# Rotary angle tables computed on GpSimd, their sines placed amid the chunks, and the second projection unit's weight splits put late and on VectorE, in a planned hybrid attention block

## The chip, the cores and the metric

The kernel runs on one core of a Trainium2 chip. The metric is the device time of one execution in microseconds. The profile is one further execution of the same program.

The engines are named as the profile names them: PE is TensorE (matmuls; PEld is its weight load), DVE is VectorE, ACT is ScalarE, POOL is GpSimd, and SP is SyncE, which issues the transfers. Each engine runs its own instructions strictly in the order in which they stand.

## What is computed

One decoder layer on x of 1024 tokens by 1024 features, in float32:

```python
mod = silu(c) @ w_ada + b_ada
sh_a, sc_a, gt_a, sh_m, sc_m, gt_m = split(mod, 6)
h = rms_norm(x, g_attn_pre) * (1 + sc_a) + sh_a
proj = h @ w_in
qa, ka, va, qb, kb, vb = split(proj)
qa, ka, qb, kb = partial_rope(each, cos, sin)
oa = banded_attention(qa, ka, va, 127, sink)
ob = dilated_mixture_attention(qb, kb, vb)
y = concat(rms_norm(oa), rms_norm(ob)) @ w_out
x = x + gt_a * rms_norm(y)
h = rms_norm(x) * (1 + sc_m) + sh_m
x = x + gt_m * rms_norm(square(relu(h @ w_up)) @ w_down)
```

`cos` and `sin` are those of position times eight fixed frequencies. They turn the first 16 of each head's 64 dimensions.

## The kernel before, in words

**Precision.** A matmul takes operands rounded to fp32r. The kernel keeps each operand as a high part (a rounding copy on ACT) and a low part (a subtraction on DVE or POOL, original minus high part) and multiplies high by high, high by low and low by high. So every weight and activation tile is "split": one ACT instruction, then one on DVE or POOL.

**A planner sets the order.** The function `hybrid_block` does not issue instructions directly. It hands steps to `Sched` with `op`: an engine (or two to choose from), an assumed duration in microseconds, the code that emits the instructions, the steps it depends on, counted resources that it takes and gives (`takes`, `gives`: buffers of a ring, PSUM banks), and a priority. `Sched.run` plays a clock forward and always places the step that can start first, so the assumed durations and the dependencies decide the order on every engine. For a step with two engines it picks the one that would end it first. On the chip each engine then runs its fixed list, with semaphores between the engines.

**x phase (x_block, lines 574 to 597).** Eight blocks of 128 tokens of x arrive. For each one ACT squares it with a row sum (L578); DVE scales the sum (L417, `rs_t`); POOL takes the power of minus one half (L420, `rstd`); DVE or ACT multiplies the block by it (L584 or L583, below "the scaling"); PE transposes it in two groups of four (L591), and DVE or ACT copies each group from PSUM into `xnT` (L595).

**Chunk phase (mod_chunk, lines 601 to 628).** Feature chunk k (of 8) of the normalized activations needs a scale `g_a` and a shift `s_a`. DVE computes each by a 1024-long product with row sum (L606, below "the gemv", two per chunk), ACT then writes the chunk's high part `hw` (L618) and the full value (L621), and DVE the low part (L624). With these goes the split of the first unit's weights for chunk k: ACT L490, DVE L495.

**The projection.** It has six units of 384 columns. In the first unit (`first_unit`) PE takes the chunks as they come: for each of chunks 0 to 5, all eight token blocks into eight accumulators `acc`, first two matmuls of each block with the high part (L747, L748) and then one with the low part (L750). Chunks 6 and 7 follow together, token block by token block. The other units (`proj_tile`, PSUM tiles `pj`) go token block by token block over all eight chunks, one set of three matmuls (L747, L748, L750) per chunk. `next_unit_w` asks for a unit's weights, and `split_w` (lines 487 to 501) splits them; for units 1 to 5 the low part could be on DVE or POOL.

**Evacuation of a projected block (evac, lines 646 to 740).** ACT writes the high part of v (L660), DVE its low part (L665); DVE turns the rotary dimensions by `cosw` and `sinw` (L676, L678, L680, below "the turn"); ACT and DVE split q and k (`sp`, `sk`: L687, L688; L692, L693); PE transposes them (`pq` L700, `pk` L712) through the one PSUM bank `px`; ACT writes `qt` (L705) and ACT or DVE `kt` (L726). Then scores (`s_ps`, L975), minimum with mask (L993, DVE), exponential (L1000, ACT), reciprocal (L1003, DVE) and normalization (L1005, POOL) follow.

**Rotary tables.** Eight angles for each of the 8 x 128 positions are 64 elements per partition. A product (L553), two rounds of range reduction (L556, L557, and L559 with L560 for each of 12 parts of two pi) and four closing steps (L566 to L569) make `ang` and `kq`, all on DVE with low priority (8); two sines on ACT (L636, L637) follow behind `e_full`, which is the last chunk's full value, and a negation on DVE (L640). The exponential in L638 only brings the table of the exponential back.

## Time and profile before

| what | us |
|---|---|
| three timed runs | 1180.21, 1184.89, 1187.25 |
| their median | 1184.89 |
| the profiled execution | 1177.44 |
| its span in the trace | 1175.3 |
| PE busy in the span | 1121.8 |
| DVE, ACT, POOL busy | 885.0, 670.4, 232.2 |

The profiled execution's time is 2.1 us more than its span, and 7.5 us less than the median of the three timed runs.

A row of the timeline has the start, the duration, the engine, the line in the code, the operation, the output and input tiles with shapes, and a count where equal neighbours are merged; in brackets stands how long the engine sat idle just before, and what ended the wait. Starts follow each other more closely than durations say, since an instruction's tail overlaps the next. A row of the windows view has, for a stretch of time, the busy time of PE, PEld, DVE, ACT and POOL with their instruction counts, then the granted PE clock (1.00 is full speed), the DMA share and GB/s.

### The profile page before, as it was taken

Reading aid. Unit: us, or ns where it says so; the run is one execution under the profiler, and the core shown is the slowest. Engines: PE = TensorE matmul, PEld = TensorE weight load, DVE = VectorE, ACT = ScalarE, POOL = GpSimd, SP = SyncE. Lnnn points to the kernel's source line nnn. Section 1 sums busy time; section 2 is a strip of 40 time slices with the busy share of each in tenths; the row PEclk is TensorE's granted clock in tenths of the full one; section 3 lists DMA queues with packets and bytes.
Section 4 is the critical chain, followed back from the end, with each engine's and each line's share of the span. In section 5 each row is a group of like instructions: output and inputs, shape, how many; then the busy total and the mean of one; then the engine's idle time right before and its main releaser. Section 6 shows DMA issues by size and latency. Waiting matters only on the chain.

```text
span 1175.3 us, 17156 instructions
## 1 busy us (share of the span) xinstructions
PE 1121.8 (95%) x5964; PEld 975.4 (83%) x5964; DVE 885.0 (75%) x1812; ACT 670.4 (57%) x1400; POOL 232.2 (20%) x279
## 2 busy tenths in 40 slices
PE   5889999999999989999899999999999999999996
PEld 4889999899988877888688888888888888888885
DVE  8978787676798986668979765489653796636998
ACT  7767666565667776667667524473225733246542
POOL 2334474554744341111000000000000000000002
PEclk9989999999999999999999999999999999999998
DMA  9602223132223224465485147932268411575103
GB/s 338 230 31 78 77 84 117 53 97 84 76 59 110 82 64 126 154 205 226 144 334 191 36 139 257 337 100 90 93 221 304 143 47 54 202 287 198 37 19 143
DMA packets 77542, 166.51 MB, mean 142 GB/s; under 512 B 6800, under 2 KB 27408, under 8 KB 77456
## 3 DMA queue, kind: packets, MB, share of 16 engines
q1 hardware_dynamic: 77456, 165.42, 41.3%
q8 instruction: 47, 0.77, 0.3%
q14 instruction: 39, 0.32, 0.1%
HBM read 137.08 MB, written 28.31 MB: 141 GB/s over the span
## 4 chain that ended last, share of the span: by engine, by line
PE 62%; DVE 10%; ACT 3%; issue 3%; POOL 2%; DMA 1%; SPq 0%; DVEq 0%; POOLq 0%; ACTq 0%
PE mlp_ps L1751 16%; PE mlp_ps L1752 16%; PE mlp_ps L1750 16%; PE pj L747 2%; PE pj L750 2%; PE pj L748 2%; PE s_ps L975 1%; DMA o_sb<-o_dram 1%; DVE hw L1521 1%; PE y_ps L1326 1%; PE y_ps L1328 1%; PE o_ps L1120 1%; PE y_ps L1327 1%; DVE x_sb L1852 1%; DVE ph L1096 1%
## 5 line engine op out<-in xcount | busy, mean ns | idle before, releaser
L1750 PE MATMUL mlp_ps<-hw 128*128 128x512 f32 x896 | 349.7, 390 | 1.2 <-ACT hw L1512 1.2
L1751 PE MATMUL mlp_ps<-hw 128*128 128x512 f32 x896 | 348.7, 389 | 1.1 <-DVE hw L1518 1.1
L1752 PE MATMUL mlp_ps<-hw 128*128 128x512 f32 x896 | 348.6, 389 | 0.0
L1750 PEld LDWEIGHTS mlp_ps<-hw 128*128 128x128 f32 x896 | 168.2, 188 | 36.8 <-ACT hw L1512 1.6
L1751 PEld LDWEIGHTS mlp_ps<-hw 128*128 128x128 f32 x896 | 168.2, 188 | 36.7 <-DVE hw L1518 1.4
L1752 PEld LDWEIGHTS mlp_ps<-hw 128*128 128x128 f32 x896 | 168.2, 188 | 34.9
L1521 DVE TENSOR_TENSOR hw<-w,hw 128x1024 fp32r<-128x1024 f32 x96 | 114.7, 1223 | 91.7 <-ACT hw L1514 91.5
L1514 ACT CAST hw<-w 128x1024 fp32r<-128x1024 f32 x96 | 97.4, 1046 | 129.8 <-PE mlp_ps L1752 97.5
L1850 POOL TENSOR_TENSOR st<-st,nhalf 128x1 f32<-128x1 f32 x8 | 7.8, 978 | 601.9 <-DVE st L1848 601.9
L747 PE MATMUL pj<-w_hl,hw 128*128 128x384 f32 x320 | 118.3, 370 | 4.6 <-DVE sk L693 4.6
L750 PE MATMUL pj<-w_hl,hw 128*128 128x384 f32 x320 | 108.1, 338 | 0.0
L748 PE MATMUL pj<-w_hl,hw 128*128 128x384 f32 x320 | 107.9, 337 | 0.0
L1514 ACT CAST hw<-u 128x1024 fp32r<-128x1024 f32 x48 | 48.7, 1052 | 64.6 <-PE mlp_ps L1752 64.6
L1096 DVE TENSOR_TENSOR ph<-pt_ps,ph 128x512 fp32r<-128x512 f32 (+1 forms) x110 | 69.1, 644 | 18.3 <-ACT ph L1092 17.8
L1521 DVE TENSOR_TENSOR hw<-u,hw 128x1024 fp32r<-128x1024 f32 x48 | 57.1, 1221 | 18.2 <-ACT hw L1514 18.2
L1005 POOL TENSOR_SCALAR p_sb<-p_sb,den 128x128 f32<-128x128 f32 (+3 forms) x64 | 49.3, 774 | 93.4 <-DVE den L1003 69.7
L1092 ACT CAST ph<-pt_ps 128x512 fp32r<-128x512 f32 (+1 forms) x110 | 59.5, 560 | 12.6 <-PE pt_ps L1081 8.7
L747 PEld LDWEIGHTS pj<-w_hl,hw 128*128 128x128 f32 x320 | 60.4, 189 | 6.3 <-issue 2.9
L1808 DVE TENSOR_TENSOR yacc<-yacc,mlp_ps 128x512 f32<-128x512 f32 x96 | 62.2, 684 | 3.3 <-PE mlp_ps L1752 3.3
L1000 ACT ACTIVATE p_sb<-p_sb,mn 128x128 f32<-128x128 f32 (+3 forms) x64 | 50.0, 781 | 21.8 <-DVE mn L993 17.8
L748 PEld LDWEIGHTS pj<-w_hl,hw 128*128 128x128 f32 x320 | 60.6, 189 | 1.2 <-issue 0.2
L750 PEld LDWEIGHTS pj<-w_hl,hw 128*128 128x128 f32 x320 | 60.1, 188 | 0.0
(205 smaller groups left out, 2176.8 us busy)
## 6 DMA issues: line engine op xcount, KB each, us to landing
hw<-s_dram SPq DMA_DIRECT2D x84, 512.0 KB, 4.5
wa_st<-in_w_ada SPq DMA_DIRECT2D x32, 512.0 KB, 4.1
w<-in_w_up SPq DMA_DIRECT2D x32, 512.0 KB, 4.9
w<-in_w_down SPq DMA_DIRECT2D x32, 512.0 KB, 7.8
s_dram<-hw SPq DMA_DIRECT2D x28, 512.0 KB, 5.0
w_st<-in_w_in SPq DMA_DIRECT2D x48, 192.0 KB, 3.8
x_sb<-in_x SPq DMA_DIRECT2D x16, 512.0 KB, 5.2
wa<-in_ada_t SPq DMA_DIRECT2D x16, 512.0 KB, 8.0
```

The lines of the kernel that those rows point to most:

```text
L747: T.matmul(ps, hw[:, tb, 0, t], w[:, 0], start=(k == 0), stop=False)
L748: T.matmul(ps, hw[:, tb, 0, t], w[:, 1], start=False, stop=False)
L750: T.matmul(ps, hw[:, tb, 1, t], w[:, 0], start=False, stop=(k == KC - 1))
L1000: A.activation(rec.p[qi], rec.p[qi], AF.Exp, bias=b["mn"][:, m:m + 1], scale=-1.0, accum_out=b["den"][:])
L1092: A.copy(b["ph"][:, 0, :w], b["pt"][:, :w])
L1096: V.tensor_tensor(b["ph"][:, 1, :w], b["pt"][:, :w], b["ph"][:, 0, :w].bitcast(F32), ALU.subtract)
L1514: A.copy(out[j][0], flat(src[j]))
L1521: V.tensor_tensor(out[j][1], flat(src[j]), out[j][0].bitcast(F32), ALU.subtract)
L1750: T.matmul(ps[m][:], sh, mh, start=starts and k == 0, stop=False, **kw)
L1751: T.matmul(ps[m][:], sh, ml_, start=False, stop=False, **kw)
L1752: T.matmul(ps[m][:], sl, mh, start=False, stop=k == 3, **kw)
L1808: e = op("DVE", t_dv(512), lambda: V.tensor_tensor(y(), y(), ps[m][:], ALU.add), [e, ml.e_y[tb, n]], gives=gives, prio=1)
```

## The change

It has five edits:

1. The range reduction of the rotary angles moves from DVE to POOL, instruction by instruction, with an assumed 0.38 us each; of the four closing steps only the clamp remains there (L569 of the changed file).
2. ACT takes over the rest: a sine with scale minus one replaces the negation, an absolute value (L638) and a sine with bias pi/2 replace the three other closing steps. The block stands behind the full value of chunk 4 instead of 7, with priority 0.
3. The low part of unit 1's weights goes to DVE alone, and waits for the low part of the last chunk (`e_hl[KC - 1]`).
4. The assumed cost of the POOL power goes from 0.18 + 0.165 w to 0.4 + 0.165 w, and that of the square to 1.14.
5. One more small constant is set at the start (`halfpi`).

```diff
-        return op("POOL", 0.18 + 0.165 * w, lambda: G.tensor_tensor(dst, box[0][:, :w], nhalf[:, :w], ALU.pow),
+        return op("POOL", 0.4 + 0.165 * w, lambda: G.tensor_tensor(dst, box[0][:, :w], nhalf[:, :w], ALU.pow),
...
+        elif u == 1:
+            w_e[u, k] = op("DVE", t_dv(UW), lo(V), [e, e_hl[KC - 1]], gives=[(r_wst, 1)], prio=3)
...
-    steps = [lambda: V.tensor_tensor(ang[:], posf[:].unsqueeze(2).to_broadcast([P, TB, 8]),
+    steps = [lambda: G.tensor_tensor(ang[:], posf[:].unsqueeze(2).to_broadcast([P, TB, 8]),
...
-            steps += [lambda part=part: V.tensor_scalar(km[:], kq[:], -part, 1.0, ALU.mult, ALU.mult),
-                      lambda: V.tensor_tensor(ang[:], ang[:], km[:], ALU.add)]
+            steps += [lambda part=part: G.tensor_scalar(km[:], kq[:], -part, 1.0, ALU.mult, ALU.mult),
+                      lambda: G.tensor_tensor(ang[:], ang[:], km[:], ALU.add)]
...
-        e = op("DVE", 0.12, f, [e, e_c], prio=8)
+        e = op("POOL", 0.38, f, [e, e_c], prio=8)
...
-        V.tensor_scalar(ang[:], ang[:], 3.1415925, -3.1415925, ALU.min, ALU.max)
-        V.tensor_scalar(kq[:], ang[:], -1.0, None, ALU.mult)
-        V.tensor_tensor(kq[:], kq[:], ang[:], ALU.max)
-        V.tensor_scalar(kq[:], kq[:], -1.0, float(np.pi / 2), ALU.mult, ALU.add)
-    e = op("DVE", 0.8, f_ang, [e], prio=8)
+        G.tensor_scalar(ang[:], ang[:], 3.1415925, -3.1415925, ALU.min, ALU.max)
+    e = op("POOL", 0.4, f_ang, [e], prio=8)
...
-        e = op("ACT", t_sb(D) + AP_COST, f_sq, [x_e[tb]], prio=2)
+        e = op("ACT", 1.14, f_sq, [x_e[tb]], prio=2)
...
         A.activation(sinw[:, :, 1], ang[:], AF.Sin)
-        A.activation(cosw[:], kq[:], AF.Sin)
-        A.activation(ang[:], kq[:], AF.Exp)
-    e = op("ACT", 3.0, f_sin, [e_ang, e_full[0]], prio=8)
-    e_rope = op("DVE", 0.15, lambda: V.tensor_scalar(sinw[:, :, 0], sinw[:, :, 1], -1.0, None, ALU.mult), [e],
-                prio=8)
+        A.activation(sinw[:, :, 0], ang[:], AF.Sin, scale=-1.0)
+        A.activation(kq[:], ang[:], AF.Abs)
+        A.activation(cosw[:], kq[:], AF.Sin, bias=halfpi[:], scale=-1.0)
+        A.activation(ang[:], kq[:], AF.Exp, scale=-1.0)
+    e_rope = op("ACT", 3.3, f_sin, [e_ang, e_full[4]], prio=0)
```

The planner then lays the instructions anew. Line numbers of the changed file are one to three higher around these places.

POOL's list at the start of the program, before: the eight powers `rstd` of the x phase stand first, and seven low parts of unit 1's weights follow.

```order
L420 ISA
L420 TENSOR_TENSOR rstd<-rs_t,nhalf 128x1 x8
L495 TENSOR_TENSOR w_hl<-w_st,w_hl 128x384 x7
L860 TENSOR_SCALAR ada_acc<-wa_st,cond 128x512
L864 TENSOR_SCALAR wa_st<-wa_st,cond 128x512
```

The same place now:

```order
L556 ISA
L556 TENSOR_TENSOR ang<-posf,head 128x64
L559 TENSOR_SCALAR kq<-ang 128x64
L560 TENSOR_SCALAR kq<-kq 128x64
L562 TENSOR_SCALAR km<-kq 128x64
L563 TENSOR_TENSOR ang<-ang,km 128x64
L562 TENSOR_SCALAR km<-kq 128x64
L421 TENSOR_TENSOR rstd<-rs_t,nhalf 128x1
L563 TENSOR_TENSOR ang<-ang,km 128x64
L562 TENSOR_SCALAR km<-kq 128x64
L563 TENSOR_TENSOR ang<-ang,km 128x64
L421 TENSOR_TENSOR rstd<-rs_t,nhalf 128x1
```

Six rotary instructions now stand ahead of the first power and 25 ahead of the eighth; five follow behind it. The seven splits of weights have left this place.

DVE's list where the last chunk is finished, before: `hw` is the low part of a chunk (the second one shown is the last chunk's), `w_hl_662` the one low part of unit 1 that DVE had, and the others are rotary steps.

```order
L624 TENSOR_TENSOR hw_126<-xnT_159,hw_126 128x8x128
L611 TENSOR_TENSOR g_a_72<-g_a_72,head_65 128x1
L559 TENSOR_SCALAR km_163<-kq_162 128x64
L495 TENSOR_TENSOR w_hl_662<-w_st_633,w_hl_662 128x384
L560 TENSOR_TENSOR ang_161<-ang_161,km_163 128x64
...
L569 TENSOR_SCALAR kq_162<-kq_162 128x64
L624 TENSOR_TENSOR hw_126<-xnT_159,hw_126 128x8x128
L640 TENSOR_SCALAR sinw_77<-sinw_77 128x8x8
```

The same place now. `w_hl_646` is the last split of unit 0, `w_hl_659`, `w_hl_672` and `w_hl_678` are chunks 0, 1 and 2 of unit 1; `acc_426` is the first token block that is evacuated.

```order
L624 TENSOR_TENSOR hw_127<-xnT_160,hw_127 128x8x128 x2
L496 TENSOR_TENSOR w_hl_659<-w_st_538,w_hl_659 128x384
L676 TENSOR_TENSOR ra_717<-acc_426,cosw_77 128x64
...
L496 TENSOR_TENSOR w_hl_672<-w_st_548,w_hl_672 128x384
...
L993 ISA mn_920 128x1
L496 TENSOR_TENSOR w_hl_678<-w_st_582,w_hl_678 128x384
L496 TENSOR_TENSOR w_hl_705<-w_st_640,w_hl_705 128x384
```

The rotary steps are gone from between the last two low parts, and the splits of unit 1 stand behind the last one: two at the start of the evacuations, and six (`w_hl_678` is the first of them) behind all eight turns of unit 0. From the first set of unit 2's first token block on, the lists of PE before and now are the same to the end (4459 of 5072 rows), and those of the other engines are the same from the same part of the program on.

More of the change, by code (lines that the diff above doesn't have):

```diff
@@ L362, in hybrid_block @@
     nhalf = const.tile([P, KC], F32, name="nhalf")
+    halfpi = const.tile([P, 1], F32, name="halfpi")
     cond = const.tile([P, KC], F32, name="cond")
@@ L509, in hybrid_block @@
         load_w(0, k)
-    e_init = op("DVE", 0.3, lambda: (V.memset(ones[:], 1.0), V.memset(nhalf[:], -0.5)), prio=0)
+    e_init = op("DVE", 0.3, lambda: (V.memset(ones[:], 1.0), V.memset(nhalf[:], -0.5), V.memset(halfpi[:], float(np.pi / 2))), prio=0)
     e = op("ACT", 0.1, lambda: A.activation(cond[:], c_raw, AF.Exp, scale=-1.0), [e_c], prio=0)
@@ L552, in hybrid_block @@
     km = p0.tile([P, TB, 8], F32, name="km")
-    steps = [lambda: V.tensor_tensor(ang[:], posf[:].unsqueeze(2).to_broadcast([P, TB, 8]),
+    steps = [lambda: G.tensor_tensor(ang[:], posf[:].unsqueeze(2).to_broadcast([P, TB, 8]),
                                      inv_f.unsqueeze(1).to_broadcast([P, TB, 8]), ALU.mult)]
     for inv, parts in ((1.0 / (TWO_PI * 4096), COARSE), (1.0 / TWO_PI, FINE)):
-        steps += [lambda inv=inv: V.tensor_scalar(kq[:], ang[:], inv, ROUND, ALU.mult, ALU.add),
-                  lambda: V.tensor_scalar(kq[:], kq[:], -ROUND, 1.0, ALU.add, ALU.mult)]
+        steps += [lambda inv=inv: G.tensor_scalar(kq[:], ang[:], inv, ROUND, ALU.mult, ALU.add),
+                  lambda: G.tensor_scalar(kq[:], kq[:], -ROUND, 1.0, ALU.add, ALU.mult)]
         for part in parts:
-            steps += [lambda part=part: V.tensor_scalar(km[:], kq[:], -part, 1.0, ALU.mult, ALU.mult),
-                      lambda: V.tensor_tensor(ang[:], ang[:], km[:], ALU.add)]
+            steps += [lambda part=part: G.tensor_scalar(km[:], kq[:], -part, 1.0, ALU.mult, ALU.mult),
+                      lambda: G.tensor_tensor(ang[:], ang[:], km[:], ALU.add)]
     e = e_pos
     for f in steps:
-        e = op("DVE", 0.12, f, [e, e_c], prio=8)
+        e = op("POOL", 0.38, f, [e, e_c], prio=8)
     def f_ang():
-        V.tensor_scalar(ang[:], ang[:], 3.1415925, -3.1415925, ALU.min, ALU.max)
-        V.tensor_scalar(kq[:], ang[:], -1.0, None, ALU.mult)
-        V.tensor_tensor(kq[:], kq[:], ang[:], ALU.max)
-        V.tensor_scalar(kq[:], kq[:], -1.0, float(np.pi / 2), ALU.mult, ALU.add)
-    e = op("DVE", 0.8, f_ang, [e], prio=8)
+        G.tensor_scalar(ang[:], ang[:], 3.1415925, -3.1415925, ALU.min, ALU.max)
+    e = op("POOL", 0.4, f_ang, [e], prio=8)
     e_ang = e
@@ L597, in x_block @@
                            gives=[(r_t, 1)], prio=2))
-    e_hh, e_hl, e_full = {}, {}, [None]
+    e_hh, e_hl, e_full = {}, {}, {}
     def mod_chunk(k):
@@ L625, in mod_chunk @@
         e_hh[k] = op("ACT", t_sb(S) + 2 * AP_COST, hi, [e1, e2] + e_xn, prio=0)
-        e = e_full[0] = op("ACT", t_sb(S) + 2 * AP_COST, full, [e_hh[k]], prio=0)
+        e = e_full[k] = op("ACT", t_sb(S) + 2 * AP_COST, full, [e_hh[k]], prio=0)
         e_hl[k] = op("DVE", t_dv(S), lo, [e], prio=0)
```

## Prediction

> **What bounds the kernel now.** I read the page, then the windows, then PE's waits and its timeline at the start, then DVE's and POOL's lists around the longest wait. PE bounds the kernel, and the start and one later stretch are where it doesn't run:
>
> ```profile
> span 1175.3 us, 17156 instructions
> ...
> PE 1121.8 (95%) x5964; PEld 975.4 (83%) x5964; DVE 885.0 (75%) x1812; ACT 670.4 (57%) x1400; POOL 232.2 (20%) x279
> ```
> ```profile
> 80.00:100.00 20.00, 17.47 (x142) 16.65 (x141) 17.20 (x65) 16.36 (x56) 5.59 (x9) 1.00 0.05 11
> ...
> 100.00:152.00 52.00, 52.00 (x385) 50.51 (x384) 38.67 (x135) 35.50 (x101) 25.16 (x30) 1.00 0.33 95
> ```
>
> From 100 to 152 us PE never stops. The lists of all engines become the same again behind unit 1's projection; PE reaches that point at 153.7 us. So I count what PE loses up to there, before and now, and the difference is the gain: what follows is the same list with PE as its bound, only shifted. PE's timeline of before:
>
> ```profile
> 25.46 0.69 PE L747 MATMUL acc<-w_hl,hw 128*128 128x384 f32 x1 [1.81 <-ACT hw L618]
> 25.95 0.52 PE L748 MATMUL acc<-w_hl,hw 128*128 128x384 f32 x1
> ...
> 55.78 0.45 PE L747 MATMUL acc<-w_hl,hw 128*128 128x384 f32 x1 [1.71 <-ACT hw L618]
> 56.06 0.34 PE L748 MATMUL acc<-w_hl,hw 128*128 128x384 f32 x1
> 61.92 0.69 PE L750 MATMUL acc<-w_hl,hw 128*128 128x384 f32 x1 [5.52 <-DVE hw L624]
> 62.40 0.52 PE L747 MATMUL acc<-w_hl,hw 128*128 128x384 f32 x1
> ...
> 65.60 0.41 PE L748 MATMUL acc<-w_hl,hw 128*128 128x384 f32 x1
> ...
> 66.20 0.33 PE L748 MATMUL acc<-w_hl,hw 128*128 128x384 f32 x1
> 66.38 0.33 PE L750 MATMUL acc<-w_hl,hw 128*128 128x384 f32 x1
> ...
> 71.80 0.34 PE L747 MATMUL pj<-w_hl,hw 128*128 128x384 f32 x1
> ...
> 153.70 0.41 PE L747 MATMUL pj<-w_hl,hw 128*128 128x384 f32 x1
> ```
>
> PE waits 1.71 us for the last chunk's high part and 5.52 us for its low part. Behind that its clock is low: ten matmuls from 62.40 to 65.60 are 0.32 us apart, later ones 0.173. With the first at 61.92 (0.48 to the next) and the last that is 10 x 0.147 + 0.31 + 0.1 = 1.9 us more. With the 2.5 us that PE lacks between 80 and 100, before loses 1.71 + 5.52 + 1.9 + 2.5 = 11.7 us behind the first matmul at 25.46.
>
> Why the last chunk is late, DVE's and POOL's timelines say:
>
> ```profile
> 47.90 0.56 DVE L495 TENSOR_TENSOR w_hl<-w_st,w_hl 128x384 fp32r<-128x384 f32 x1
> 48.37 1.29 DVE L606 CUSTOM_DVE_ANT_0 wa<-wa,cond_b,bb 128x1024 f32<-128x1024 f32 x1
> ...
> 49.57 2.04 DVE L606 CUSTOM_DVE_ANT_0 wa<-wa,cond_b,bb 128x1024 f32<-128x1024 f32 x1
> ...
> 51.54 2.04 DVE L624 TENSOR_TENSOR hw<-xnT,hw 128x1024 fp32r<-128x1024 f32 x1
> ...
> 54.48 1.35 DVE L495 TENSOR_TENSOR w_hl<-w_st,w_hl 128x384 fp32r<-128x384 f32 x1
> ...
> 60.65 1.22 DVE L624 TENSOR_TENSOR hw<-xnT,hw 128x1024 fp32r<-128x1024 f32 x1
> 61.78 0.19 DVE L640 TENSOR_SCALAR sinw<-sinw 128x64 f32<-128x64 f32 x1
> ```
> ```profile
> 48.60 6.82 POOL L495 TENSOR_TENSOR w_hl<-w_st,w_hl 128x384 fp32r<-128x384 f32 x4 [28.22 <-ACT w_hl L490]
> 56.21 1.00 POOL L495 TENSOR_TENSOR w_hl<-w_st,w_hl 128x384 fp32r<-128x384 f32 x1 [0.79 <-DVE km L559]
> 57.76 1.95 POOL L495 TENSOR_TENSOR w_hl<-w_st,w_hl 128x384 fp32r<-128x384 f32 x2 [0.55 <-ACT w_hl L490]
> ```
>
> A gemv costs 1.20 us of DVE, a low part 1.13, a split 0.47; while POOL splits, each costs about 0.8 more (2.04 against 1.29, 1.35 against 0.56), and POOL's four take 1.7 each instead of 1.0. The two engines shut each other out. Then come the rotary steps, ahead of the last low part at 60.65.
>
> **The change part by part.**
>
> *The wait removed.* No split and no rotary step stands on DVE's way to the last chunk any more. From the end of the first shift `s_a` to that of the last, DVE has 14 gemvs, six low parts, six splits and small ones: 14 x 1.20 + 6 x 1.13 + 6 x 0.47 + 0.5 = 26.9 us. ACT's high part, a split and the full value, then DVE's low part, follow: 1.15 + 0.4 + 1.15 + 1.13 and steps between, 4.0.
>
> *The start.* POOL's small instructions are bounded by these rows:
>
> ```profile
> 6.72 0.55 POOL L420 TENSOR_TENSOR rstd<-rs_t,nhalf 128x1 f32<-128x1 f32 x1 [6.30 <-DVE rs_t L417]
> ...
> 18.87 1.51 POOL L420 TENSOR_TENSOR rstd<-rs_t,nhalf 128x1 f32<-128x1 f32 x1 [1.37 <-DVE rs_t L417]
> ...
> 61.96 0.70 POOL L860 TENSOR_SCALAR ada_acc<-wa_st,cond 128x512 f32<-128x512 f32 x1 [2.26 <-DVE sinw L640]
> ...
> 79.31 0.37 POOL L1005 TENSOR_SCALAR p_sb<-p_sb,den 128x128 f32<-128x128 f32 x1 [10.52 <-DVE den L1003]
> ```
> ```profile
> 3.74 0.16 DVE L547 CAST posf<-posi 128x8 f32<-128x8 int32 x1
> ...
> 11.91 0.75 DVE L584 TENSOR_SCALAR x_sb<-x_sb,rstd 128x1024 f32<-128x1024 f32 x1
> 12.58 0.68 DVE L595 COPY xnT<-pxt 128x512 f32<-128x512 f32 x1
> ...
> 18.70 1.28 DVE L606 CUSTOM_DVE_ANT_0 wa<-wa,cond_b,bb 128x1024 f32<-128x1024 f32 x1
> ```
>
> From 0.37 us for 128 elements and 0.70 for 512, 64 elements come to about 0.31, and with the step between dependent ones 0.39 (my estimate). Ahead of the eighth power stand 25 of them and seven powers: from 3.9 us, 25 x 0.39 + 8 x 0.55 = 14.2, so it ends at 18.0 if nothing holds POOL. It ended at 20.38 before, and there DVE's gemv of 18.70 held it by 0.96. Seven scalings of 0.67 and a gemv can hold POOL's list by up to 5.9, to 23.9. I take 22.5, nearer the upper end, because the scalings wait for these very powers and so meet the rotary steps queued around them. DVE's eighth scaling, a split and the gemv of `s_a` follow in its list: 22.5 + 0.1 + 0.67 + 0.07 + 0.47 + 1.20 = 25.0. With ACT's high part PE starts at about 26.4, 1.0 later than before. Bounds: 1 us earlier, because DVE is rid of 20 rotary steps here, to 3 later.
>
> *The last chunk.* Five rotary steps of POOL still fall among DVE's gemvs; at the 0.8 that a split six times as long took, less for their size, I give 1.0 in all. The last shift ends at 25.0 + 26.9 + 1.0 = 52.9, the low part at 56.9. Before, PE would have taken it at 54.3 (the wait of 55.78 began at 54.07), 28.8 behind its start; now that is 55.2. PE waits 1.8 us (bounds 0.5 and 3.5).
>
> *The sines.* They take ACT between chunks 4 and 5:
>
> ```profile
> 42.79 1.24 ACT L618 ACTIVATE hw<-xnT,s_a,g_a 128x1024 fp32r<-128x1024 f32 x1 [1.29 <-DVE s_a L606]
> ...
> 58.11 1.28 ACT L636 ACT_TABLE_LOAD   x1
> 60.05 0.26 ACT L636 ACTIVATE sinw<-ang 128x64 f32<-128x64 f32 x1 [0.65 <-DVE ang L566]
> ```
>
> Two table loads of 1.28 and five small ones at some 0.2 are 3.7 us. ACT idles about 1.3 a chunk (the row at 42.79), so chunk 5's high part slips some 2 us, and PE, which takes that chunk 4.16 us (24 x 0.173) after the last, still finds it there. They cost nothing, and the time that ACT had to give them behind the last chunk is free. If ACT's slack is gone they cost up to 2 at the last chunk, inside its bound.
>
> *The late weights.* Before, POOL's last split of unit 1 ended at 59.7 (the row at 57.76), and PE went from the last `acc` to `pj` at 71.80 without a wait. Now six of eight chunks stand behind all turns of unit 0 on DVE:
>
> ```profile
> 72.55 0.22 DVE L676 TENSOR_TENSOR ra<-acc,cosw 128x64 f32<-128x64 f32 x1
> ...
> 73.40 0.35 DVE L665 TENSOR_TENSOR v_hl<-acc,v_hl 128x64 fp32r<-128x64 f32 x2
> 73.67 0.28 DVE L692 TENSOR_TENSOR sp<-acc,sp 128x128 fp32r<-128x128 f32 x1
> ...
> 74.20 0.21 DVE L676 TENSOR_TENSOR ra<-acc,cosw 128x64 f32<-128x64 f32 x1
> ```
>
> A turn is 0.85, a pair of v 0.27, the q and k splits 0.53. Up to chunk 2's weights DVE has 8 x 0.85 + 8 x 0.27 + 4 x 0.53, a first mask, two copies and three splits: 13.4, so to 70.3. PE has 45 matmuls, transposes and two sets: 9.7, to 66.6. It waits 3.7, of which transposes and scores fill 0.9: 2.8 lost. From chunk 2 to 7 DVE has 8.6 (five splits, six masks, four q and k splits), PE 6.3: 2.3 lost. Together 5.1 (bounds 2 and 7, for what ACT adds or the planner's fill hides). DVE's list sets the pace there, so a low clock of PE is mostly hidden; I give it 0.5. Its bounds are nought, since the gap of 1.71 at 55.78 brought no slow matmuls, and 1.9, since those from 25.46 on are slow (0.52) after a half-busy x phase and a gap of only 1.81. The Trainium skill (TensorE: Matmul & The Clock Gate, "What's actually happening") says that the clock falls after an idle window of about 3.4 us; by that the term is nought and the time 0.5 less, but the row at 25.46 goes against it.
>
> *Behind it* PE has a whole token block of `pj` with its weights ready as filler, so of the 2.5 between 80 and 100 I leave 0.3.
>
> **The sum.** Now 1.0 + 1.8 + 5.1 + 0.5 + 0.3 = 8.7 against 11.7: a gain of 3.0. The profiled execution, 1177.4, becomes 1174.4; it lies 7.5 below the median of the runs, so I forecast 1181.9.
>
> **The rivals.**
>
> *Everything hides (faster).* POOL keeps pace in the x phase (start 0.5 earlier), the last chunk waits 0.8, the late weights 2.5: 2.8 lost, a gain of 8.9, 1176.0. For it: 20 small instructions leave DVE there. Against it: powers now queue behind rotary steps.
>
> *POOL and DVE shut each other out in the x phase (slower).* My 22.5 holds 4.5 us of blocking over 33 POOL instructions, 0.14 each. At 0.23 each the gain is gone; at 0.41 the change is slower by over 0.5%; at 0.45 it is 10.4 worse, 1192.3. For it: POOL's splits at 48.60 lost 0.7 each. Against it: they met a DVE with no gaps and long instructions; in the x phase copies from PSUM and waits lie between. The Trainium skill (SBUF — State Buffer, "Who interferes with whom") has it that one of the two blocks fully for the whole instruction where DVE has two SBUF inputs or a 2-port mode; the 2.04 of the row at 49.57 agrees, and it speaks against moving small steps to POOL while DVE scales x.
>
> *The lead is given back (same).* The evacuations of unit 0 cost DVE and ACT the same, so that PE's early finish ends in waits of 8 us instead of 5.1: 1184.9. For it: DVE is busy for 17.20 of 20 between 80 and 100. Against it: PE waits little there.
>
> **How the numbers follow.** A measurement here can tell about 0.5%, 5.9 us, from no change. Forecast 0.50, given back 0.11, everything hides 0.30, shut out 0.09. The first two lie within 5.9 us of 1184.9. With all bounds at their best 10.2 us are gained (1174.7), with all at their worst 5.2 lost (1190.1); all at once is unlikely, so the range ends at 1189.0. Faster 0.30, same 0.61, slower 0.09.
>
> **What would show it.** In the profile after, PE's first `acc` matmul near 26.4, with POOL's eighth power ending near 22.5; no 5 us wait for L624's `hw`, but one under 3.5; PE waits on the weights (`w_hl`, then `pj`) of some 5 us between 63 and 80; the first set of unit 2 at about 150.7 instead of 153.7. I am wrong if POOL's list ends the x phase past 26, if `pj` starts without waits, or if the lead at unit 2 doesn't reach the end.

## The result and the profile after

| | before | after |
|---|---|---|
| median of the timed runs, us | 1181.91 | 1176.42 |
| profiled execution, us (span) | 1177.44 (1175.3) | 1179.2 (1177.0) |
| a second profiled execution, us (span) | 1182.08 (1179.8) | 1171.23 (1169.4) |

The ratio of the times, after to before, is 0.9958 (95% interval 0.9943 to 0.9974), and 0.9964 (0.9947 to 0.9981) when the changed kernel was timed again with the experiments: 4 to 5 us faster. Both intervals lie below 1, but the gain is less than the half per cent (5.9 us) that the prediction took as the least that can be told from no change. The forecast was a gain of 3.0. One timed run of the kernel before, of 1853 us, is not in the ratio.

The two first profiled executions stand the other way round than the medians, and the second pair does not. A span is therefore no measure here. What can be compared is when PE reaches the same place in its list, so each kernel got four marks: its first `acc` matmul, DVE's first turn (the start of the evacuations), unit 2's first `pj` set, and the 97th set counted from there, behind which all kernels of this study have the same list of PE.

PE's timeline of the changed kernel, first execution (start, duration, operation; in brackets the idle time before and what ended it):

```profile
27.50 0.69 PE L747 MATMUL acc<-w_hl,hw 128*128 128x384 f32 x1 [2.02 <-ACT hw L618]
...
54.91 0.44 PE L750 MATMUL acc<-w_hl,hw 128*128 128x384 f32 x1 [0.46 <-DVE hw L624]
...
57.80 0.69 PE L750 MATMUL acc<-w_hl,hw 128*128 128x384 f32 x1 [2.10 <-DVE hw L624]
58.29 0.52 PE L747 MATMUL acc<-w_hl,hw 128*128 128x384 f32 x1
...
61.17 0.35 PE L747 MATMUL acc<-w_hl,hw 128*128 128x384 f32 x1
...
68.11 0.34 PE L747 MATMUL pj<-w_hl,hw 128*128 128x384 f32 x1
...
69.69 0.34 PE L700 MATMUL pq<-ident_r,sp 128*128 128x128 f32 x2 [0.36 <-DVE sp L692]
70.46 0.44 PE L975 MATMUL s_ps<-kt,qt 128*128 128x128 f32 x2 [0.43 <-DVE sk L693]
...
71.99 0.50 PE L975 MATMUL s_ps<-kt,qt 128*128 128x256 f32 x2 [0.75 <-DVE mn L993]
...
80.36 0.41 PE L1078 MATMUL pt_ps<-head,p_sb 128*128 128x128 f32 x2 [1.34 <-DVE den L1003]
...
150.81 0.41 PE L747 MATMUL pj<-w_hl,hw 128*128 128x384 f32 x1
```

The same of its second execution:

```profile
25.09 0.44 PE L747 MATMUL acc<-w_hl,hw 128*128 128x384 f32 x1 [2.02 <-ACT hw L618]
...
52.51 0.45 PE L750 MATMUL acc<-w_hl,hw 128*128 128x384 f32 x1 [0.21 <-DVE hw L624]
...
55.41 0.44 PE L750 MATMUL acc<-w_hl,hw 128*128 128x384 f32 x1 [2.09 <-DVE hw L624]
...
59.59 0.34 PE L700 MATMUL pq<-ident_r,sp 128*128 128x128 f32 x2 [0.78 <-ACT v_hl L660]
...
66.99 0.34 PE L700 MATMUL pq<-ident_r,sp 128*128 128x128 f32 x2 [0.64 <-DVE sp L692]
67.76 0.44 PE L975 MATMUL s_ps<-kt,qt 128*128 128x128 f32 x2 [0.43 <-DVE sk L693]
...
69.29 0.50 PE L975 MATMUL s_ps<-kt,qt 128*128 128x256 f32 x2 [0.74 <-DVE mn L993]
...
77.62 0.41 PE L1078 MATMUL pt_ps<-head,p_sb 128*128 128x128 f32 x2 [1.34 <-DVE den L1003]
...
148.42 0.41 PE L747 MATMUL pj<-w_hl,hw 128*128 128x384 f32 x1
```

The wait of over 5 us for the last low part is gone; 2.3 to 2.6 us are left, in two pieces. Behind it PE waits 2.9 to 3.9 us in small pieces. None is a wait for weights, and `pj` starts without one (68.11): what comes late are the q and k splits, the mask and the reciprocal, which stand with the late weights in DVE's list.

The kernel before, second execution:

```profile
53.56 0.44 PE L750 MATMUL acc<-w_hl,hw 128*128 128x384 f32 x1 [1.95 <-DVE hw L624]
...
55.70 0.69 PE L747 MATMUL acc<-w_hl,hw 128*128 128x384 f32 x1 [1.70 <-ACT hw L618]
...
61.83 0.69 PE L750 MATMUL acc<-w_hl,hw 128*128 128x384 f32 x1 [5.12 <-DVE hw L624]
```

All marks, in us of each kernel's profiled execution ("waits" are those for the last chunk from 52 us on):

| kernel | first acc | waits | first turn | unit 2 | 97th set | ratio to before (95%) |
|---|---|---|---|---|---|---|
| before | 25.46 | 7.2 | 63.00 | 153.70 | 261.15 | |
| before, again | 25.44 | 8.8 | 62.91 | 154.79 | 263.56 | 1.0014 (0.9999 to 1.0029) |
| after | 27.50 | 2.6 | 58.89 | 150.81 | 259.83 | 0.9958 (0.9943 to 0.9974) |
| after, again | 25.09 | 2.3 | 56.25 | 148.42 | 255.81 | 0.9964 (0.9947 to 0.9981) |
| E1 free splits | 26.44 | 2.4 | 57.91 | 152.60 | 261.48 | 0.9969 (0.9955 to 0.9983) |
| E2 rotary on DVE, late | 26.07 | 2.3 | 61.99 | 159.53 | 265.69 | 0.9998 (0.9982 to 1.0015) |
| E3 sines after chunk 2 | 26.07 | 3.0 | 58.00 | 150.64 | 259.08 | 0.9964 (0.9950 to 0.9977) |
| E4 powers first | 25.79 | 8.0 | 64.18 | 158.31 | 267.28 | 1.0052 (1.0030 to 1.0074) |
| E5 rotary on DVE, early | 29.80 | 0.7 | 59.06 | 154.19 | 257.80 | 0.9947 (0.9931 to 0.9962) |
| E6 before with edit 3 alone | 25.60 | 2.6 | 58.73 | 154.54 | 259.28 | 0.9951 (0.9935 to 0.9968) |
| E7 late, either engine | 25.20 | 2.3 | 56.66 | 146.95 | 251.56 | 0.9921 (0.9898 to 0.9945) |
| E8 sines last | 25.72 | 2.7 | 58.82 | 150.78 | 256.94 | 0.9949 (0.9932 to 0.9965) |
| E9 E7 with sines after chunk 2 | 26.42 | 4.8 | 60.85 | 151.48 | 256.08 | 0.9930 (0.9911 to 0.9948) |
| E10 E7 with sines last | 26.25 | 3.3 | 60.79 | 153.93 | 258.64 | 0.9961 (0.9946 to 0.9976) |

(Unit 2's mark lies at the same row of PE's list in all but E1 and E5, where it stands four matmuls later, behind waits of 2.29 and 1.23 us.) Two executions of one kernel differ by up to 2.6 us at the first turn, 2.4 at unit 2 and 4.0 at the 97th set. Each experiment has one execution, so a smaller difference between two marks says nothing.

Between unit 2 and the 97th set PE's list isn't the same in all kernels, since the planner lays it anew with each edit. The kernels before and after, E3 and E4 have one list there, which takes 107.4 to 109.0 us; E2 and E6 to E10 share another, of 104.6 to 106.2; E1 (108.9) and E5 (103.6) have their own. So the times of E2 and E5 to E10 hold some 2 to 5 us that come with the other list, and only the marks up to unit 2 tell what their edits do at the start.

With the means of the two executions each, the changed kernel leads by 5.4 us at the first turn (57.57 against 62.96), by 4.6 at unit 2 (149.62 against 154.25) and by 4.5 at the 97th set (257.82 against 262.36), and its times lead by 4 to 5. So the gain of the changed kernel is made before the first turn, a little is lost in the evacuations, and the rest reaches the end.

### The profile page after: what moved, and what is told of

It reads as the page before. It is cut to its first block, busy times and chain, and to the rows that moved or that the text cites. A ratio compares the mean times of both kernels' runs of the same rounds, so it can differ in the third digit from the quotient of the medians.

```text
span 1177.0 us, 17146 instructions
## 1 busy us (share of the span) xinstructions
PE 1127.4 (96%) x5964; PEld 980.9 (83%) x5964; DVE 877.3 (75%) x1784; ACT 670.3 (57%) x1404; POOL 235.5 (20%) x302
## 4 chain that ended last, share of the span: by engine, by line
PE 72%; DVE 13%; ACT 6%; DMA 3%; issue 3%; POOL 2%; SPq 0%; DVEq 0%; POOLq 0%; ACTq 0%
PE mlp_ps L1751 16%; PE mlp_ps L1752 16%; PE mlp_ps L1750 16%; PE pj L747 3%; PE pj L750 3%; PE pj L748 3%; PE s_ps L975 2%; PE o_ps L1109 1%; PE pt_ps L1078 1%; DMA o_sb<-o_dram 1%; DMA w_st<-in_w_in 1%; PE pt_ps L1081 1%; PE y_ps L1326 1%; PE y_ps L1328 1%; DVE hw L1521 1%
## 5 line engine op out<-in xcount | busy, mean ns | idle before, releaser
L1000 ACT ACTIVATE p_sb<-p_sb,mn 128x128 f32<-128x128 f32 (+3 forms) x64 | 49.8, 779 | 18.1 <-DVE mn L993 14.3
```

## The experiments

**Second executions of both kernels.** No edit.

> The changed kernel once more, for a second profile and a second set of times beside the runs below. Theory (the lead at unit 2 is real, single profiles scatter by some us behind it): unit 2's first set again between 149 and 151 us, the time 0.3 to 0.5% below the kernel before. If a start of 27.5 us was a whim of one execution, it comes at 26.1 to 26.5 here, as it did in the two kernels that share the x phase with it.

> The kernel before once more, for a second profile. Theory: its first profiled execution was a lucky one (1177.4 us against a median of 1181.4 to 1181.9); unit 2's first set comes at 153 to 156 us, with waits of 5 us or more for the last chunk, and the span is 1178 to 1181. If the lead over the changed kernel were not there in usual executions, unit 2's first set would come at 151.

Both came as expected: 148.42 against 154.79 at unit 2. The start of 27.50 was that execution's own; here it is 25.09, and in the six further kernels with this x phase (E1, E3, E7 to E10) 25.20 to 26.44.

**E1: edit 3 undone.**

```diff
-        elif u == 1:
-            w_e[u, k] = op("DVE", t_dv(UW), lo(V), [e, e_hl[KC - 1]], gives=[(r_wst, 1)], prio=3)
```

> The changed kernel with edit 3 undone: unit 1's low parts of weights may again be on VectorE or GpSimd and wait for nothing, and the planner puts six of them on GpSimd right behind the rotary clamp, among the gemvs. Theory (the gain is what PE loses less up to unit 2, and the splits on GpSimd are the larger part of the long wait for the last chunk): each of the six costs DVE some 0.8 us, so PE's waits for the last chunk rise from 2.6 to about 7 us, a stretch of slow clock follows, and the waits and gaps of 3.5 us between 68 and 81 us go; unit 2's first set comes at about 152 instead of 150.8, and the time is 0.1 to 0.2% above the changed kernel's, about 0.3% below the kernel before. Rival (the late splits only move the loss): the last chunk waits 3 to 4 us, pj starts without waits, unit 2's first set comes at 148 to 149, and the kernel is 0.5 to 0.7% faster than before. Rival (the late splits are the whole gain): unit 2's first set at 153.7 and the time of the kernel before.

The time is 0.3% below before as in the theory, but the waits are not: 2.4 us, not 7. The premise failed. POOL's list has six splits behind the clamp, but they start late, as POOL's timeline of E1 shows:

```profile
52.83 2.79 POOL L496 TENSOR_TENSOR w_hl<-w_st,w_hl 128x384 fp32r<-128x384 f32 x2 [25.22 <-ACT w_hl L491]
```

They wait for their high parts on ACT, which has the sines at chunk 4 and is behind. In the kernel before, without sines there, POOL's splits began at 48.60. So edit 3 is not needed where ACT is late with the high parts; the experiment doesn't tell what it is worth.

**E2: the rotary steps back on DVE at low priority.** The `G.` of edit 1's steps becomes `V.`, with:

```diff
-        e = op("POOL", 0.38, f, [e, e_c], prio=8)
+        e = op("DVE", 0.12, f, [e, e_c], prio=8)
```

> The changed kernel with the rotary range reduction back on VectorE at low priority (0.12 us assumed each, clamp 0.2); the sines keep their dependence on chunk 4, and the planner now puts them later, beside the first evacuations. Theory (GpSimd's rotary steps delay the powers, and so the start, by 2.0 us; on VectorE they cost about 30 x 0.15 = 4.5 us, of which the x phase hides a third): PE's first acc matmul comes back to 25.5, the last chunk waits 3 us longer than in the changed kernel, unit 2's first set comes at 151 to 152, 0 to 1 us later, and the time is 0 to 0.1% above the changed kernel's. Rival (moving the rotary steps is what pays): last-chunk waits of over 7 us, unit 2's first set at 154 or later, the time of the kernel before. Rival (the move costs more than it brings): first matmul at 25.5, last chunk as in the changed kernel, unit 2's first set at 149.

The gain is gone, but not at the last chunk (2.3 us of waits). The planner put the last angles behind it; the clamp starts at 59.37, ACT's sines follow, and the first turn waits for them. DVE's and PE's timelines of E2:

```profile
59.37 0.20 DVE L569 TENSOR_SCALAR ang<-ang 128x64 f32<-128x64 f32 x1
...
61.99 0.23 DVE L676 TENSOR_TENSOR ra<-acc,cosw 128x64 f32<-128x64 f32 x1 [1.69 <-ACT cosw L639]
```
```profile
68.66 0.47 PE L700 MATMUL pq<-ident_r,sp 128*128 128x128 f32 x2 [4.65 <-DVE sk L693]
```

At unit 2 it is 5.3 us behind the kernel before. So E2 says that angles which come late cost what the late splits bring, not that POOL must make them; E5 tries that.

**E3: the sines after chunk 2.** `e_full[4]` becomes `e_full[2]`; PE's and POOL's orders stay.

> The changed kernel with the sine block behind the full value of chunk 2 instead of chunk 4; PE's and GpSimd's orders are unchanged. Theory (ACT never idles from chunk 4 on in the changed kernel, so the block of 3.7 us reaches the last chunk; two chunks earlier ACT still has idle time to absorb it): the last high part follows its shift by 0.1 instead of 0.5 us, the wait for the last low part falls from 2.1 to 1 us or less, unit 2's first set comes 0.8 to 1.5 us earlier, and the time is 0.1% below the changed kernel's. Rival (VectorE's list alone sets the last chunk and the sines cost nothing, as the prediction has it): the waits of 2.6 us stay, unit 2's first set at 150.8, no difference.

The rival held, as the prediction had it: waits of 3.0 us, unit 2 at 150.64, the same time.

**E4: all rotary steps behind the eighth power.** The loop that emits them stands behind the x blocks and depends on the last power (the diff is cut at the dots; the clamp moves with the loop):

```diff
-    e = e_pos
-    for f in steps:
-        e = op("POOL", 0.38, f, [e, e_c], prio=8)
...
+        e_pw.append(e)
...
+    e = e_pw[-1]
+    for f in steps:
+        e = op("POOL", 0.38, f, [e, e_c], prio=8)
```

> The changed kernel with all rotary steps of GpSimd behind the eighth power of the x phase instead of amid the powers; PE's order is unchanged. Theory (the start came 2.0 us later because the powers queue behind rotary steps and each of these meets a scaling on VectorE): the eighth power ends near 20.5 to 21 instead of 23.5, PE's first acc matmul comes at 25.3 to 25.9 instead of 27.5; the 31 rotary steps now all meet gemvs and cost VectorE about 0.06 each, 1 us in all by the last chunk more than now; since PE's pace up to the last chunk is 4.16 us a chunk, PE then waits about 1 to 2 us more there; unit 2's first set comes at about 150.3, 0 to 1 us earlier. Rival (the contention of the small steps is as dear among gemvs as a split's, 0.2 or more each): the last chunk waits 6 us or more and unit 2's first set comes at 152 or later. Rival (the start alone sets the lead): unit 2's first set at 148.8, 2 us earlier.

Slower by 0.5%. The start is 25.79 as expected, and the rival's 6 us are there, but by a way that neither theory named. POOL, DVE, ACT and PE in E4:

```profile
25.93 1.10 POOL L562 TENSOR_SCALAR km<-kq 128x64 f32<-128x64 f32 x1
...
50.82 0.24 POOL L628 TENSOR_SCALAR ang<-ang 128x64 f32<-128x64 f32 x1
```
```profile
24.39 1.27 DVE L597 CUSTOM_DVE_ANT_0 wa<-wa,cond_b,bb 128x1024 f32<-128x1024 f32 x1
...
25.60 1.33 DVE L597 CUSTOM_DVE_ANT_0 wa<-wa,cond_b,bb 128x1024 f32<-128x1024 f32 x1
```
```profile
51.10 0.26 ACT L636 ACTIVATE sinw<-ang 128x64 f32<-128x64 f32 x1 [6.43 <-POOL ang L628]
```
```profile
54.76 0.69 PE L747 MATMUL acc<-w_hl,hw 128*128 128x384 f32 x1 [6.19 <-ACT hw L609]
```

Among the gemvs 19 of the 30 rotary steps take 1.1 to 1.3 us, as long as a gemv, where one takes 0.24 with DVE idle (the row at 50.82). DVE loses only 0.06 a gemv. It is POOL that is starved: its 30 steps last from 21.8 to 51.1, ACT stands at the sine for 6.4 us with the next chunk behind it, and PE waits 6.2. The Trainium skill (SBUF — State Buffer, "Who interferes with whom") calls the shared port pair an exclusive lock; these rows agree, and they show which side pays when one engine's instructions are long and leave no gaps.

**E5: the rotary steps on DVE, early.** E2 with priority 2 instead of 8.

> The changed kernel with the whole range reduction on VectorE again, but at priority 2, so that the planner puts it between the scalings and copies of the x phase and it is done before the first shift; sines after chunk 4 and late splits as in the changed kernel. Theory (what pays is that the angles are ready early and nothing but gemvs and low parts stands on VectorE's way to the last chunk; which engine reduces them matters little): about 33 x 0.15 = 5 us on VectorE, of which its idle time in the x phase takes the larger part; the first acc matmul at 25.5 to 27, unit 2's first set at 149.5 to 151.5, the time 0.3 to 0.5% below the kernel before. Rival (GpSimd is what pays): the x phase grows by 3 us or more, the first acc matmul at 28.5 or later, unit 2's first set at 153 or later, the time of the kernel before.

The time is the theory's (0.53% below before), the head is the rival's: PE starts at 29.80, 4.3 us late. Yet it takes the last low part at 58.22 with a wait of 0.70, and the first turn is at 59.06. Of the 3.5 us that it starts later than the changed kernel's mean (26.3), 1.5 are left at the first turn (59.06 against 57.57): the wait for the last chunk took up the rest. At unit 2 no lead is left in this execution (154.19), and the time is made behind it, in E5's own list of PE. So E5 shows that the wait for the last chunk goes without POOL as well; it doesn't show what early steps on DVE are worth to the end.

**E6: the kernel before with edit 3 alone.** The two lines of E1's diff, added to the kernel before.

> The kernel before with edit 3 alone (unit 1's low parts on VectorE and behind the last chunk's). Theory (edit 3 takes the splits' 5 us off the way to the last chunk, and the rotary steps and the sines, left behind the last chunk, eat it): the wait for the last low part falls from 5.5 to 2 or 3 us, but the first turns wait for the cosine table until about 62 us, and PE waits 4 us or more behind the last acc matmul; with the late weights, unit 2's first set comes at 154 to 159, the time is within 0.2% of the kernel before. Rival (edit 3 is the gain): unit 2's first set at 151 or earlier, 0.3% faster or more. Rival (late weights are a loss of over 5 us by themselves): slower by 0.4% or more.

The time is that of the rival for which edit 3 is the gain (0.49% faster), the mark at unit 2 is the theory's, and the first turn comes at 58.73 and not at 62.

The waits for the last chunk fall to 2.6 as with all five edits. That is the disputed 5 us, and edit 3 alone takes them. The rotary steps that stayed on DVE cost nothing there: they lie in DVE's wait for the full value, which ACT writes until 54.74. In the kernel before they had held the last low part: ACT had written its full value at 57.28, and the low part began at 60.65, with three of the steps taking about 1.0 instead of 0.2 while POOL split. ACT's and DVE's timelines of before:

```profile
56.04 1.24 ACT L621 ACTIVATE xnT<-xnT,s_a,g_a 128x1024 f32<-128x1024 f32 x1
```
```profile
56.00 0.20 DVE L559 TENSOR_SCALAR km<-kq 128x64 f32<-128x64 f32 x1
56.23 1.06 DVE L560 TENSOR_TENSOR ang<-ang,km 128x64 f32<-128x64 f32 x1
```

The same place in E6, ACT's and DVE's timelines:

```profile
53.50 1.24 ACT L623 ACTIVATE xnT<-xnT,s_a,g_a 128x1024 f32<-128x1024 f32 x1
```
```profile
52.11 0.19 DVE L561 TENSOR_SCALAR km<-kq 128x64 f32<-128x64 f32 x1
...
54.77 0.20 DVE L571 TENSOR_SCALAR kq<-kq 128x64 f32<-128x64 f32 x1
54.88 1.22 DVE L626 TENSOR_TENSOR hw<-xnT,hw 128x1024 fp32r<-128x1024 f32 x1
```

By unit 2 the lead is lost (154.54), with waits for the evacuations' `qt` and `sk` in PE's timeline:

```profile
83.53 0.54 PE L714 MATMUL pk<-ident_r,sk 128*128 128x128 f32 x4 [1.42 <-ACT qt L707]
...
85.80 0.66 PE L1080 MATMUL pt_ps<-head,p_sb 128*128 128x128 f32 x2 [1.73 <-DVE sk L695]
```

The waits are less than half of the loss. Behind them PE's granted clock was low for 6.83 us, as it had been from 57.09 to 60.50; the row of the windows view of E6 has the granted clock, 0.50, behind the busy times:

```profile
84.39:91.22 6.83, 5.42 (x28) 5.45 (x29) 3.87 (x14) 3.04 (x10) 0.14 (x1) 0.50 0.00 0
```

The next table counts from PE's last wait among the `acc` rows to unit 2, in us; "slow clock" is half of what PE is busy while its granted clock is 0.50:

| kernel | in all | waits | slow clock | rest |
|---|---|---|---|---|
| before | 91.8 | 2.5 | 1.9 | 87.3 |
| before, again | 93.0 | 2.5 | 3.3 | 87.1 |
| after | 93.0 | 3.3 | 1.7 | 88.1 |
| after, again | 93.0 | 4.5 | 0 | 88.5 |
| E6 | 98.4 | 5.8 | 4.4 | 88.2 |
| E8 | 94.7 | 4.6 | 1.6 | 88.5 |

The rest is the same within 1.4 us, so waits and slow clock account for what E6 loses: 5.4 us more than the changed kernel, of which 1.3 to 2.5 are waits and 2.7 to 4.4 the clock.

The time comes back behind unit 2, in the other list. PE's timeline, of the changed kernel and of E7, which shares E6's list there:

```profile
221.05 0.41 PE L747 MATMUL pj<-w_hl,hw 128*128 128x384 f32 x1 [2.35 <-DVE sk L693]
```
```profile
215.35 0.33 PE L1078 MATMUL pt_ps<-head,p_sb 128*128 128x128 f32 x1 [1.08 <-POOL p_sb L1005]
```

The wait of 2.35, which the kernel before has too, becomes one of 1.08.

**E7: late splits on either engine.**

```diff
-            w_e[u, k] = op("DVE", t_dv(UW), lo(V), [e, e_hl[KC - 1]], gives=[(r_wst, 1)], prio=3)
+            w_e[u, k] = op(("DVE", "POOL"), (t_dv(UW), t_ptt(UW)), (lo(V), lo(G)), [e, e_hl[KC - 1]], gives=[(r_wst, 1)], prio=3)
```

> The changed kernel with edit 3 in part: unit 1's low parts still wait for the last chunk's, but may be on GpSimd or VectorE; the planner puts five of eight on GpSimd and lays PE's list from unit 2 to row 1127 in the way of the kernel before with edit 3 alone and of the kernel with the rotary steps early on VectorE, in which the wait of 2.4 us of PE for DVE's sk near 240 us is not there. Theory (two separate gains: the last chunk's wait, 4 to 5 us, carried to unit 2, and this other order behind it, 3 to 4 us): unit 2's first set at 149 to 152 us, its 97th (the first place that all kernels share again) at 254 to 256 instead of 256 to 260, and the time 0.6 to 0.8% below the kernel before, below the changed kernel's by 0.2 to 0.4%. Rival (the lead is eaten on the way, as in the kernel with edit 3 alone, since the evacuations set the pace and not PE's start): unit 2's first set at 154, its 97th at 258 to 260, the time 0.4 to 0.5% below the kernel before. Rival (splits on GpSimd beside the evacuations cost VectorE 0.8 us each again): 4 us of waits between 60 and 80, 0.2% or less below.

Both gains come at once, as the theory had it. The time is its (0.79% below before), and the marks are some 2 us earlier than it said: unit 2 at 146.95, the 97th set at 251.56. PE's waits between the last chunk and unit 2 are 1.5 us in all, where the changed kernel has 3.3 and 4.5. Its interval (0.9898 to 0.9945) lies below the changed kernel's 0.9958 and 0.9964 and just meets the first one's interval, which begins at 0.9943; it has the lowest ratio of the study, and E9's interval overlaps it.

**E8: the sines last.** `[e_ang, e_full[4]], prio=0` becomes `[e_ang, e_full[7]], prio=8`.

> The changed kernel with the sine block behind the last chunk's full value, at priority 8, as before the change; rotary steps on GpSimd, late splits. Beside the kernel before with edit 3 alone it tells what the move to GpSimd is worth. Theory (nothing that can be measured: with the splits gone, the rotary steps that DVE had at the last chunk lie in its wait for the full value, and on GpSimd they lie in idle time too): last chunk's wait 1.5 to 2.5 us, the first turn waits for the cosine table until about 58.5 us, unit 2's first set at 153 to 155, its 97th at 258 to 260, the time 0.4 to 0.6% below the kernel before. Rival (the move of the rotary steps is worth some us by itself): 0.7% or more below. Rival (the sines before the last chunk are what pays): within 0.2% of the kernel before.

0.9949, and E6 0.9951: with the splits late, the timed runs show no value in the rotary steps' move to POOL. The marks aren't the theory's: unit 2 comes at 150.78 and the 97th set at 256.94, 3.8 and 2.3 us ahead of E6. With one execution of each it stays open whether the move brings something up to there. What E8 does show is that the lead reaches unit 2 with the sines last, so their place at chunk 4 isn't what carries it.

**E9 and E10: E7 with the sines after chunk 2, and last.**

> The first of these three with the sine block behind chunk 2's full value instead of chunk 4's; PE's order is the same in both. Theory (the sines reach the last chunk by some 0.5 us at most, since VectorE's list binds there too): unit 2's first set 0 to 1 us earlier than in the first, the time the same within 0.1%. Rival (ACT without idle time from chunk 4 on is what delays the last chunk): the wait for the last low part 1 us shorter, the time 0.1 to 0.2% below the first's.

> The kernel with late splits on either engine, with its sine block moved from behind chunk 4 to behind the last chunk's full value (priority 8, as before the change). With the two kernels of sines last and splits on VectorE, and of sines after chunk 4 and splits on either engine, it tells which of the two differences is worth the 3 us between them (0.9949 and 0.9921 of the kernel before). Theory (VectorE sets the pace between 60 and 100 us, and five splits of 0.47 us on GpSimd take 2.4 us off its list): unit 2's first set at 147 to 149.5, the time 0.7 to 0.8% below the kernel before. Rival (the sines' place pays, because the first turns wait for the cosine table): unit 2's first set at 150.5 to 152, the time 0.45 to 0.55% below. Both in half: 149 to 150.5, 0.6 to 0.65%.

E9's time is E7's within the intervals, but unit 2 comes 4.5 us later, not earlier. E10 is 0.4% slower than E7 and at 153.93 at unit 2, which is beyond its rival too. At the first turn they are 4.2 and 4.1 us behind E7; 1.2 and 1.1 of it is there at the first `acc` matmul already, which is within what executions differ by. In E10 the first turn also waits 1.38 us for ACT, whose `v_hl` stands behind the sine block. The rest both lose at the last chunk, where 2.0 us gemvs are back, three in E9 and one in E10. DVE's and POOL's timelines of E9, and POOL's and DVE's of E10:

```profile
49.90 2.03 DVE L606 CUSTOM_DVE_ANT_0 wa<-wa,cond_b,bb 128x1024 f32<-128x1024 f32 x1
...
53.82 2.00 DVE L606 CUSTOM_DVE_ANT_0 wa<-wa,cond_b,bb 128x1024 f32<-128x1024 f32 x1
```
```profile
48.12 4.68 POOL L496 TENSOR_TENSOR w_hl<-w_st,w_hl 128x384 fp32r<-128x384 f32 x3 [20.54 <-ACT w_hl L491]
```
```profile
47.70 2.72 POOL L496 TENSOR_TENSOR w_hl<-w_st,w_hl 128x384 fp32r<-128x384 f32 x2 [20.29 <-ACT w_hl L491]
```
```profile
49.48 2.03 DVE L606 CUSTOM_DVE_ANT_0 wa<-wa,cond_b,bb 128x1024 f32<-128x1024 f32 x1
...
60.79 0.23 DVE L676 TENSOR_TENSOR ra<-acc,cosw 128x64 f32<-128x64 f32 x1 [1.38 <-ACT v_hl L660]
```

On POOL the planner's wait for the last low part holds in the plan alone; on the chip POOL starts a split as soon as its high part is there. With the sines moved away from chunk 4, ACT writes the high parts earlier, POOL starts at 47.70 or 48.12, and a gemv costs 2.03 instead of 1.27 again. With the sines at chunk 4 (E7) POOL starts at 51.59, as in E1 near 53, and the waits are 2.3. So in E7, E9, E10 and E1 the place of the sines acts through the start of POOL's splits.

## Why the prediction was right, and where it was not

The terms of its sum, against what the two executions of the changed kernel show (waits as in the timelines above):

| term, us | forecast | first | second |
|---|---|---|---|
| start, against 25.46 | 1.0 | 2.0 | -0.4 |
| last chunk | 1.8 | 2.6 | 2.3 |
| late weights | 5.1 | 2.9 | 3.9 |
| slow clock | 0.5 | 1.5 | 0 |
| behind it | 0.3 | 0.4 | 0.6 |
| sum (before: 11.7) | 8.7 | 9.4 | 6.4 |
| lead that follows | 3.0 | 2.3 | 5.3 |
| lead seen at unit 2, against 153.70 | | 2.9 | 5.3 |

The clock's 1.5 is the time of ten matmuls, 57.80 to 61.17 in the first execution and 1.85 in the second. The line "behind it" is what PE lacks of 50 us in these rows of the windows view, of the first and of the second execution (what it lacks between 80 and 100 us is the wait at 80.36 and counts with the weights):

```profile
100.00:150.00 50.00, 49.61 (x357) 47.46 (x357) 36.40 (x126) 32.53 (x98) 24.45 (x29) 1.00 0.36 101
```
```profile
100.00:150.00 50.00, 49.41 (x352) 47.18 (x351) 35.37 (x125) 33.02 (x100) 26.71 (x31) 1.00 0.39 112
```

The sum describes both executions to within 0.6 us. Point by point:

*The wait removed: right.* Which edit removes it the prediction left to all of them. E6 shows that edit 3 alone does, and E1 that the other four do as well, because ACT, with the sines at chunk 4, then hands POOL its splits too late to meet the gemvs. E9 and E10 show that a part of it returns when splits on POOL meet the last gemvs again. Of the two causes that the prediction named, the splits are the one that counts: the rotary steps held the last low part beside POOL's splits, and hold it no more without them (E6).

*The start: right on the mean, and with luck.* 26.3 over the two executions, for a forecast of 26.4, but neither is near it: 27.50 and 25.09. (With the six further kernels that have this x phase the mean is 26.1.) POOL's eighth power ended at 23.48 in the first execution (forecast 22.5):

```profile
21.95 1.53 POOL L421 TENSOR_TENSOR rstd<-rs_t,nhalf 128x1 f32<-128x1 f32 x1 [0.69 <-DVE rs_t L418]
```

E5 shows that the term matters less than the sum has it, since a late start shortens the wait for the last chunk.

*The last chunk: 0.5 to 0.8 too small.* It was to be done 30.5 us behind the first `acc` matmul, and came after 30.25 in both executions (57.75 and 55.35). PE was there 28.2 us behind its start, and not 28.8, so it waited longer.

*The sines: right, for the splits as they are.* E3 shows no gain from freeing ACT before the last chunk.

*The late weights: the term that was mis-sized.* The step to chunk 2's weights held: DVE was to need 13.4 us and needs 14.3 in the second execution, from 55.35 to about 69.7 (the first of the two in the row below), and PE loses 2.6 on the way (0.78, 0.64, 0.43 and 0.74) for a forecast of 2.8. The step from chunk 2 to chunk 7 was wrong: 1.3 for 2.3. The prediction also took the waits to be on weights, and it named a `pj` that starts without waits as a sign that it is wrong. That sign came (68.11). The mechanism held all the same, that DVE's list behind the last chunk sets PE's pace, but PE meets it at the q and k splits, the mask and the reciprocal that stand beside the weights.

```profile
69.18 1.03 DVE L496 TENSOR_TENSOR w_hl<-w_st,w_hl 128x384 fp32r<-128x384 f32 x2
```

*The clock: near both of its bounds.* It cost 1.5 and nothing, for bounds of 1.9 and nought. Behind a gap of 2.10 (57.80) the next nine steps are 0.32 apart; behind one of 2.09 (55.41) they are 0.17. The last section has what decides it. The prediction gave the clock a term behind the last chunk alone; in E6 it is the larger part of a lost lead.

*The lead is carried: shown.* 4.6 at unit 2, 4.5 at the 97th set, 4 to 5 in the times. The rival that it is given back in the evacuations holds for E6, not for this change.

*The other rivals.* "Everything hides" didn't happen: 6 to 9 us are still lost. That its time, 1176.0, is so near to the measured 1176.42 is chance, because it was reckoned from 1184.89. "POOL and DVE shut each other out in the x phase" has its mechanism (E4) and not its place: in the x phase DVE leaves gaps, and the powers came at most 1 us later than forecast.

*The median.* Of the 5.5 us between the forecast of 1181.9 and the 1176.42 that came, 3.0 are the median of the kernel before, which is 1181.91 over more runs and not 1184.89. About 1.6 are the lead, 4.6 for 3.0. The remaining 0.9 is less than the interval of the ratio leaves open (1.8 us either way). The list behind the 97th set takes 913.6 to 917.2 us over the four executions of these two kernels, nearly as much apart as the whole gain.

*The sums.* The wait for the last chunk is 56.9 less 55.2, which is 1.7 and not 1.8. The worst case of 5.2 us lost needs 1.5 for what lies "behind it", a bound that the prediction doesn't name. The sum of 8.7 came near the measured ones also because its errors offset each other: 0.5 to 0.8 too little at the last chunk, 1.2 to 2.2 too much for the weights.

What stays open: why DVE's order in E6 makes PE wait 1.42 and 1.73 us where the changed kernel doesn't, and whether the rotary steps' move to POOL is worth something, for which the marks of E8 and E6 speak and their times don't.

## What to carry to other kernels

Where two engines shut each other out, move the work of the one off the place where the other is what everybody waits for, and see that it stays off: a planner's order without a semaphore behind it moves with any change on a third engine, as the sines showed. Count a wait of the bound engine with what its clock does behind it: in E6 the slow clock cost more than the waits had added. Measure a change in the head of a program at one row of the bound engine's list, in two executions, and not by the span of one. A block on an engine that others wait for must not wait for a starved engine's last step.

## What the hardware showed beside it

A 128x64 step on POOL takes 0.24 to 0.32 us when DVE is idle or between short instructions, and 1.1 to 1.3 between gemvs of 1.27, which lengthen to 1.33. A 128x384 split on POOL (1.0 alone) takes 1.7 beside them in the kernel before (four in 6.82), and the gemv 2.03 or 2.04. So in these rows a gemv loses 0.06 beside POOL's short step and 0.75 beside its long one, and POOL loses 0.7 to 1.0 to a gemv with either.

PE's clock was low after a gap of 1.62 us in E8 and after one of 2.10 in the changed kernel, and full after 2.09 in its second execution. PE's timeline of E8:

```profile
56.09 0.69 PE L750 MATMUL acc<-w_hl,hw 128*128 128x384 f32 x1 [1.62 <-DVE hw L624]
```

The granted clock in the traces changes only at instants that lie a multiple of 3.41 us apart. The next rows of the windows view are cut there: two neighbouring stretches of the changed kernel in its first execution, and two in its second.

```profile
54.34:57.75 3.41, 0.90 (x4) 0.47 (x3) 1.74 (x3) 3.38 (x6) 0.00 (x0) 1.00 0.77 250
57.75:61.16 3.41, 3.35 (x10) 3.36 (x11) 2.54 (x11) 0.87 (x4) 0.00 (x0) 0.50 0.19 58
```
```profile
50.42:53.83 3.41, 2.68 (x14) 2.04 (x13) 2.04 (x4) 3.41 (x5) 0.00 (x0) 1.00 0.44 109
53.83:57.24 3.41, 1.83 (x10) 1.84 (x11) 2.55 (x7) 1.82 (x6) 0.00 (x0) 1.00 0.44 156
```

In the first execution most of the gap falls into one stretch, in which PE is busy for 0.90 of 3.41 us, and the clock is 0.50 in the next. In the second an instant at 53.83 cuts the gap in two, PE is busy for 2.68 and 1.83, and the clock stays. From 15 us on, the 14 traces have 4578 such stretches at full clock. Of the 55 in which PE was busy for less than 45%, 53 were followed by the low clock; of the 124 between 45 and 75%, 14; of the 4399 above, none. Once low, the clock came back only behind a stretch in which PE was busy for 80% or more. (The profile models where a matmul ends, so the shares are approximate.) So these traces tell the two gaps apart by where they fall, and not by their length.

The Trainium skill (TensorE: Matmul & The Clock Gate, "What's actually happening") speaks of an idle window of about 3.4 us; the length agrees with these rows, which show that PE need not be idle in all of it.
